# Attention inside a gate projection: transposes of p three steps behind their scores, pv products four, with a fifth buffer for p

## The chip, the cores and the metric

The kernel runs on one core of one Trainium2 chip. The metric is the device time of one execution in microseconds (us). The times shown are the median, lowest and highest of three executions; a profile was taken of one execution.

## The reference, cut to what matters

One layer of an encoder, for a prompt of 1024 rows and a sample of 64 rows (1088 rows in all, model width 1024, 8 heads of width 64). Only the attention matters here:

```python
def mixer(xn, conv_prefix, attn_fn, w_in, w_conv, w_conv_out, w_attn_out, w_out):
    proj = xn @ w_in
    cb, cc, ch, q, k, v, ga, gb = jnp.split(proj, ...)
    ya = (cb * causal_conv(cc * ch)) @ w_conv_out
    o = attn_fn(heads(q), heads(k), heads(v))
    yb = o.reshape(B, L, ATT_DIM) @ w_attn_out
    merged = jax.nn.sigmoid(ga) * ya + jax.nn.sigmoid(gb) * yb
    return merged @ w_out, ...

def band_attend(q, k, v, q_pos, k_pos, rel_bias):
    s = jnp.einsum('bqhd,bkhd->bhqk', q, k) * (HEAD_DIM ** -0.5)
    allowed = ...          # own chunk of 64 rows and the 8 chunks before it
    s = jnp.where(allowed, s + bias, NEG_INF)
    p = jax.nn.softmax(s, axis=-1)
    return jnp.einsum('bhqk,bkhd->bqhd', p, v)
```

A SwiGLU feed-forward part follows; the change does not touch it.

## The kernel before, in words

Every product is made from two halves of each operand (a high part and a low part in a reduced 32-bit format), so that a product of 128 contraction rows costs three matmuls (L333, L334, L335). The part of the program that the change touches has two streams of work, which share TensorE (PE).

The first stream is the gate projections `g`: ten blocks of 128 columns, each in four pieces of 272 rows, 24 matmuls of 128x272 a piece. Their sums are copied out by ScalarE (ACT, L815) and stored.

The second is the attention, a Python generator of steps. A step is one tile of one head: 8 heads with 9 tiles each (t = 0 to 7 are 128 rows of the prompt, t = 8 is the 64 rows of the sample), so 72 steps in the order (0,0), (0,1) ... (7,8). In this text `s5_6` is the scores of head 5, tile 6, `t5_6` the transposes of the same tile, and s_0 or t_7 means that tile in any head. A step's work:

- `scores` (L892 on): the matmuls L907 and L908 into the PSUM tile `s`; VectorE (DVE, L865) adds the bias, writes the sum to the SBUF tile p and finds its extreme in one pass; ScalarE (L875) makes the exponential in place in p and adds up its rows. A tile has 128 (t = 0), 256, 384, 512 or 640 columns (t = 4 to 7), and 576 for the sample.
- `transposed` (L920 on): TensorE transposes p, 128 columns at a time, into a PSUM tile `t` (L954; L926 and L929 for the sample). ScalarE copies it out as the high part of `pt` (L128), VectorE subtracts to get the low part (L129), and with that the PSUM buffer is free. For t = 8 the reciprocal of the head's row sums follows (L935) and a transpose of it, `rt` (L937).
- `values` (L958 on): for each pair of tiles the products with v, `pv` (L979, and L966 for the sample), copied and added up (L881 to L883) and stored in `o_d` by a DMA (L886).

The scores, the transposes and `rt` take their PSUM tiles from one pool, `patt`, with two buffers in all (the tag "att"). The gates have three PSUM banks of their own, pv one. The SBUF tile p rotates through four buffers.

How far the three parts of a step lie apart is set in `attention` (L1007 on): turn i of its loop issues the scores of step i, the transposes of step i-2 and the pv products of step i-3. `between()` runs after each gate piece and takes 3.15 turns on average (PER). Before the last two gates, `for _ in steps: pass` (L1061) takes all turns that are left; then the attention's pools are closed and the loads of `u` and the output of the attention (`ob`, L1072 to L1088) are issued, whose products `ya` and `yb` come behind the last gate. A scheduler then orders the instructions of each engine by its own estimate of times; that is why the orders below are not simply those of the code. Once ordered, each engine takes its instructions strictly in that order.

Of the kernel before, what the change touches and what calls it, by code (L numbers as in the profile page):

```python
# [8 lines left out]
F32 = mybir.dt.float32  # L9
# [6 lines left out]
P = 128  # L16
# [50 lines left out]
def encoder_kernel(ctx: ExitStack, tc: tile.TileContext, ins, outs):  # L67
# [58 lines left out]
    def split(hi, lo, src):  # L126

        a = act.copy(hi, src)  # L128
        b = vec.tensor_tensor(lo, src, hi.bitcast(F32), op=ALU.subtract)  # L129
        return a.ins, b.ins  # L130
# [626 lines left out]
    for n in range(len(units)):  # L757
# [21 lines left out]
        for _ in r:  # L779
            if n < 2 and si in (2 + n, 5 + n):  # L780
                i = 2 * n + si // 5
# [23 lines left out]
    at_pool = att_stack.enter_context(tc.tile_pool(name="at_pool", bufs=2, reuse_waits="tile"))  # L805
# [24 lines left out]
    def head_load(h):  # L830
        q = []
        for l in range(2):
            qq = qp.tile([P, T], F32R, tag=f"q{l}", name=f"qd{h}_{l}", bufs=2 + l)
            for j in range(2):
                nc.sync.dma_start(qq[j * HD : (j + 1) * HD].bitcast(F32), q_d[h, :, l])
            q.append(qq)
        k = hd_pool.tile([P, TP], F32R, tag="k", name=f"kd{h}")
        ks = hd_pool.tile([P, CACHE + TS], F32R, tag="ks", name=f"ksd{h}", bufs=1)

        for l in range(2):  # L840
            ls = slice(l * HD, (l + 1) * HD)
            src = k_d[h, :, l]
            for e in range(2):
                nc.sync.dma_start(k[ls, 512 * e : 512 * e + 512].bitcast(F32), src[:, 576 * e : 576 * e + 512])
            nc.sync.dma_start(ks[ls, :CACHE].bitcast(F32), src[:, T:])
            nc.sync.dma_start(ks[ls, CACHE:].bitcast(F32), src[:, 512:576])
        v = hd_pool.tile([P, 8, P], F32R, tag="v", name=f"vd{h}")
        nc.sync.dma_start(v.bitcast(F32), v_d[h, :TP].rearrange("(b p) e -> p b e", p=P))
        vs = hd_pool.tile([P, 5, P], F32R, tag="vs", name=f"vsd{h}", bufs=1)
        nc.sync.dma_start(vs[:, :4].bitcast(F32), v_d[h, TP : TP + CACHE].rearrange("(b p) e -> p b e", p=P))  # L850
        nc.sync.dma_start(vs[:TS, 4].bitcast(F32), v_d[h, TP + CACHE :])
        b = bb[:, h % 2]
        near = bias_d[h, 127 : 127 + P * 383].rearrange("(p n) -> p n", n=383)
        far = bias_rows(h, 0, 384)
        nc.sync.dma_start(b[:HD, :384], far[:HD])
        nc.sync.dma_start(b[HD:, HD:384], far[HD:, HD:])
        nc.sync.dma_start(b[:HD, 384:576], near[:HD, :192])
        nc.sync.dma_start(b[HD:, 384:], near[HD:, :256])
        heads[h] = (q, k, ks, v, vs, b)

    def softmax(s, ps, bias, sm, nm):

        rows = s.shape[0]
        mx = at_pool.tile([P, 1], F32, tag="mx", name=f"mx{nm}", bufs=3)[:rows]
        vec.tensor_tensor_reduce(  # L865
            out=s if len(ps.shape) == 2 else s.rearrange("p (a b) -> p a b", a=2),
            in0=ps,
            in1=bias if len(ps.shape) == 2 else bias.rearrange("p (a b) -> p a b", a=2),
            scale=-1.0,
            scalar=3e38,  # L870
            op0=ALU.add,
            op1=ALU.min,
            accum_out=mx,
        )
        act.activation(s, s, AF.Exp, bias=mx, scale=-1.0, accum_out=sm)  # L875
# [16 lines left out]
    def scores(h, t):  # L892
        q, k, ks, v, vs, bias = heads[h]
        ps = patt.tile([P, 2, 512], F32, tag="att", name=f"s{h}_{t}")
        s = at_pool.tile([P, 640], F32, tag="s", name=f"p{h}_{t}", bufs=4)
        if t < 8:
            nb = min(t + 1, 5)
            k0, n, r = (t - nb + 1) * P, nb * P, P
            q0 = t * P if t < 4 else t * P + TS
        else:  # L900
            k, k0, n, r = ks, 0, CACHE + TS, TS
            q0 = 512
        parts = 2 if n > 512 else 1
        w = n // parts
        for i in range(parts):
            ksl = slice(k0 + i * w, k0 + (i + 1) * w)
            mm(ps[:r, i, :w], q[0][:, q0 : q0 + r], k[:, ksl], start=True, stop=False)  # L907
            mm(ps[:r, i, :w], q[1][:, q0 : q0 + r], k[:, ksl], start=False, stop=True)  # L908
        b0 = 640 - n if t < 8 else 0
        if t == 0:  # L910
            sums[h] = sm2[:, h % 2]
        sm = sums[h]
        softmax(
            s[:r, :n], ps[:r, :, :w] if parts == 2 else ps[:r, 0, :w], bias[:r, b0 : b0 + n], sm[:r, t : t + 1],
            f"{h}_{t}",
        )
        return s
# [3 lines left out]
    def transposed(h, t, s):  # L921
        tp = patt.tile([P, 2, 512], F32, tag="att", name=f"t{h}_{t}").rearrange("p a b -> p (a b)")
        if t == 8:
            pt = at_pool.tile([P, 2, 5, TS], F32R, tag="pts", name=f"pts{h}", bufs=1)
            for i in range(4):
                nc.tensor.transpose(  # L926
                    tp[:, i * TS : (i + 1) * TS], s[:TS, i * P : (i + 1) * P], ident[:TS, :TS]
                )
            nc.tensor.transpose(tp[:TS, 512 : 512 + TS], s[:TS, 512:576], ident[:TS, :TS])  # L929
            split(pt[:, 0, :4, :], pt[:, 1, :4, :], tp[:, : 4 * TS].rearrange("p (b t) -> p b t", t=TS))  # L930
            split(pt[:TS, 0, 4, :], pt[:TS, 1, 4, :], tp[:TS, 512 : 512 + TS])
            pts[h, 4] = pt

            sm = sums.pop(h)
            vec.reciprocal(sm, sm)  # L935
            tr = patt.tile([P, 2, 512], F32, tag="att", name=f"rt{h}")[:9, 0, :P]
            nc.tensor.transpose(tr, sm, ident)  # L937
            rows = at_pool.tile([P, P], F32, tag="rows", name=f"rows{h}", bufs=1)[:9]
            act.copy(rows, tr)
            for e in range(2):  # L940
                nc.gpsimd.dma_start(
                    rc_d[h, e * HT : e * HT + 512].rearrange("(t p) -> t p", p=P), rows[4 * e : 4 * e + 4]
                )
                c = e * HT + 512
                nc.gpsimd.dma_start(rc_d[h : h + 1, c : c + 32], rows[8:9, 32 * e : 32 * e + 32])
            return
        g, j = divmod(t, 2)
        if j == 0:
            pts[h, g] = at_pool.tile([P, 2, 6, 256], F32R, tag="pt", name=f"pt{h}_{g}")
        pt = pts[h, g]  # L950
        nb = min(t + 1, 5)
        b0 = t - nb + 1 - max(0, 2 * g - 4)
        for i in range(nb):
            nc.tensor.transpose(tp[:, i * P : (i + 1) * P], s[:, i * P : (i + 1) * P], ident)  # L954
        src = tp[:, : nb * P].rearrange("p (b t) -> p b t", t=P)
        js = slice(j * P, (j + 1) * P)
        split(pt[:, 0, b0 : b0 + nb, js], pt[:, 1, b0 : b0 + nb, js], src)
# [49 lines left out]
    def attention():  # L1007
        order = [(h, t) for h in range(NH) for t in range(9)]
        done = []
        for i in range(len(order) + 3):  # L1010
            if i < len(order):
                h, t = order[i]
                if t == 3 and h + 1 < NH:
                    head_load(h + 1)
                if h + 1 == NH and t in (3, 5):
                    o_early(t // 4)
                done.append(scores(h, t))
            if 0 <= i - 2 < len(order):
                transposed(*order[i - 2], done[i - 2])
            if i >= 3:  # L1020
                h, t = order[i - 3]
                if t % 2 or t == 8:
                    values(h, t)
            yield
# [34 lines left out]
    for i in range(4, len(GATES)):  # L1059
        gate_w[i] = next_w()  # L1060
        if i == len(GATES) - LAST:  # L1061
# [5 lines left out]
            for nm, pad in (("u", 56), ("ob", 48)):  # L1067
                uo.tile([P, pad], F32, name=f"pad_{nm}")
                t = uo.tile([P, 2, 4 * T + 8], F32R, name=nm)[:, :, : 4 * T]
# [27 lines left out]
    for m0 in range(0, 8, 2):  # L1097
        for m in (m0, m0 + 1):
# [3 lines left out]
            for o, n in PIECES:  # L1102
                t = sg["ga", m, o]
# [5 lines left out]
        for m in (m0, m0 + 1):  # L1109
# [3 lines left out]
            for o, n in PIECES:  # L1113
                t, z = sg.pop(("ga", m, o)), sg.pop(("gb", m, o))
# [7 lines left out]
                h, a = o // HT, 512 - o % HT  # L1122
# [468 lines left out]
    order = [(i + 4 * h, d) for g in range(2) for h, d in ((0, 0), (1, 0), (1, 1), (0, 1)) for i in (2 * g, 2 * g + 1)]  # L1591
    homes = [(hp, "snap")] * 3 + [(hp0, "snap"), (hp0, "sa")] + [(hp, "sa")] * 4 + [(hp, "hs")]
    bufs = {(hp, "hs"): 1, (hp, "snap"): 3, (hp, "sa"): 4, (hp0, "snap"): 1, (hp0, "sa"): 1}
    for n, (i, d) in enumerate(order):
        if n < len(homes):
            pool, tag = homes[n]
# [28 lines left out]
    for b, ks in enumerate(blocks):  # L1625
        first, final = b == 0, b == len(blocks) - 1
        nk = blocks[b + 1] if not final else []
        for g in range(2):
# [28 lines left out]
            for si, js in turns:  # L1657
                p, ht = STEPS[si], hts[base + si]
                key = {1: "A", 6: "A", 5: "A", 3: "A", 2: "B", 7: "D", 4: "D"}[p]
                for j in js:  # L1660
                    i = 2 * g + j
                    if (key, j) not in ps:
                        ps[key, j] = psD.tile(
                            [P, 512], F32, tag="A" if key == "A" else "BD", name=f"{key}{b}_{i}",
                            bufs=2 if key == "A" else 4,
                        )
                    t = ps[key, j]
                    for k, kp in enumerate(ks):
# [7 lines left out]
                    h, d, fresh = {  # L1676
                        1: (0, 0, 1), 2: (0, 0, 0), 6: (1, 0, 1), 7: (1, 1, 1), 5: (1, 1, 0), 4: (1, 0, 0), 3: (0, 1, 1),
                    }[p]
# [79 lines left out]
```

## Time and profile before

| | |
|---|---|
| time, median of 3 (lowest to highest) | 1472.06 us (1471.79 to 1472.19) |
| the profiled execution: own time, span | 1471.79 us, 1469.7 us |
| mean granted TensorE clock of that execution | 0.998 |
| busy in the span: PE, DVE, ACT, POOL | 1455.4, 984.1, 679.9, 136.5 us |
| first scores, first gate matmul behind the last pv | 370.20 us, 551.00 us |
| first `ya` matmul, first `yb` matmul | 571.82 us, 583.84 us |

The page gives, for one execution, the busy time of each engine and its share of the span, the span in 40 slices, the chain of work that ended last, and the costliest groups of instructions. The trace behind it gives each instruction with its start, its duration and what ended the idle time ahead of it. Matmuls are pipelined, so their durations overlap; what a matmul costs is read from the distance of two starts.

### The profile page before, as it was taken

The page shows a single profiled execution, that of the slowest core. Times are in us where ns is not written, and L with a number is a line of the kernel's source. Part 1 is how long each engine was busy: PE and PEld are TensorE (multiplying, and loading weights), DVE is VectorE, ACT ScalarE, POOL GpSimd, SP SyncE. Part 2 cuts the span into 40 slices and gives each one's busy share as a digit, 9 for nine tenths or more (in the row PEclk, how much of TensorE's full clock was granted, in tenths as well). Part 3 has the DMA queues.
Part 4 walks back from the last instruction along what each step waited for, and adds up shares of the span by engine and source line. Part 5 has one row for each costly group of instructions (what it writes and reads, how often), then busy time and mean ns, then how long its engine had stood idle before and what let it go on. Part 6 is the DMA issues. An engine that isn't in the chain of part 4 may idle for free.

```text
span 1469.7 us, 26408 instructions
## 1 busy us (share of the span) xinstructions
PE 1455.4 (99%) x10176; PEld 1366.7 (93%) x10176; DVE 984.1 (67%) x1856; ACT 679.9 (46%) x1391; POOL 136.5 (9%) x249
## 2 busy tenths in 40 slices
PE   9999999999999999999999999999999999999997
PEld 6899999999989899998889999999999999888886
DVE  7975465641677775763588767766666768957676
ACT  7654433422777776531355444444444445512223
POOL 1400010001111111000100111110011111000000
PEclk9999999999999999999999999999999999999999
DMA  8686522237776757534432443443344449877675
GB/s 285 181 277 225 178 88 88 66 115 228 209 193 179 182 168 244 164 119 136 154 108 80 153 168 139 168 151 123 122 152 168 147 166 303 287 233 239 223 268 205
DMA packets 163134, 260.26 MB, mean 177 GB/s; under 512 B 18785, under 2 KB 98849, under 8 KB 163009
## 3 DMA queue, kind: packets, MB, share of 16 engines
q1 hardware_dynamic: 142080, 192.79, 42.1%
q0 software_dynamic: 19776, 63.70, 12.1%
q10 hardware_dynamic: 1152, 2.10, 0.4%
q8 instruction: 80, 1.31, 0.4%
q14 instruction: 46, 0.37, 0.1%
HBM read 170.67 MB, written 89.70 MB: 177 GB/s over the span
## 4 chain that ended last, share of the span: by engine, by line
PE 94%; DVE 3%; ACT 1%; DMA 1%; issue 1%; SPq 0%; ACTq 0%; DVEq 0%
PE Ab L269 9%; PE Aa L269 8%; PE A L1671 8%; PE Db L269 4%; PE Da L269 4%; PE D L1671 4%; PE g L335 3%; PE g L334 3%; PE g L333 3%; PE Agb L269 2%; PE B L1671 2%; PE wo L1163 2%; PE Bb L269 2%; PE Ba L269 2%; PE wo L1165 2%; PE wo L1164 2%
## 5 line engine op out<-in xcount | busy, mean ns | idle before, releaser
L333 PE MATMUL g<-xn,wp 128*128 128x272 f32 x320 | 93.7, 293 | 0.0
L335 PE MATMUL g<-xn,low 128*128 128x272 f32 x320 | 93.4, 292 | 0.0
L334 PE MATMUL g<-xn,wp 128*128 128x272 f32 x320 | 92.7, 290 | 0.0
L128 ACT CAST ring<-w2r 128x512 fp32r<-128x512 f32 (+1 forms) x78 | 43.2, 588 | 97.9 <-PE A L1671 49.9
L865 DVE CUSTOM_DVE_ANT_0 p<-s,bb 128x640 f32<-128x640 f32 (+5 forms) x72 | 47.4, 660 | 38.5 <-PE s L908 37.2
L1671 PE MATMUL A<-ring,low 128*128 128x512 f32 x264 | 72.4, 389 | 0.0
L1671 PE MATMUL A<-ring,ht 128*128 128x512 f32 x264 | 72.4, 390 | 0.0
L129 DVE TENSOR_TENSOR low<-rawa,wa 128x512 fp32r<-128x512 f32 x55 | 37.7, 687 | 41.4 <-ACT wa L128 41.4
L335 PEld LDWEIGHTS g<-xn,low 128*128 128x128 f32 x320 | 60.3, 189 | 0.5
L333 PEld LDWEIGHTS g<-xn,wp 128*128 128x128 f32 x320 | 60.3, 189 | 0.5
L334 PEld LDWEIGHTS g<-xn,wp 128*128 128x128 f32 x320 | 60.2, 188 | 0.5
L1671 PEld LDWEIGHTS A<-ring,low 128*128 128x128 f32 x264 | 49.6, 188 | 10.4
L1671 PEld LDWEIGHTS A<-ring,ht 128*128 128x128 f32 x264 | 49.3, 188 | 10.6 <-ACT acc L1681 0.6
L269 PE MATMUL Aa<-tt,wa 128*128 128x272 f32 x352 | 57.8, 285 | 0.9 <-ACT sa_Q L257 0.9
L269 PE MATMUL Aa<-mg,wa 128*128 128x272 f32 x352 | 57.8, 286 | 0.5 <-DVE sa L1324 0.5
L269 PE MATMUL Ab<-mg,wb 128*128 128x272 f32 x352 | 57.9, 285 | 0.0
L129 DVE TENSOR_TENSOR ring<-w2r,ring 128x512 fp32r<-128x512 f32 (+1 forms) x78 | 48.9, 645 | 13.4 <-ACT ring L128 13.4
L269 PE MATMUL Ab<-tt,wb 128*128 128x272 f32 x352 | 57.8, 286 | 0.0
L875 ACT ACTIVATE p<-p,mx 128x640 f32<-128x640 f32 (+5 forms) x72 | 50.8, 706 | 11.5 <-DVE mx L865 10.2
L128 ACT CAST wa<-rawa 128x512 fp32r<-128x512 f32 x55 | 34.0, 621 | 47.4 <-PE Ab L269 33.3
L128 ACT CAST wb<-rawb 128x512 fp32r<-128x512 f32 x55 | 33.9, 621 | 38.8 <-PE Aa L269 24.5
L1163 PE MATMUL wo<-low,mg 128*128 128x512 f32 x128 | 50.9, 397 | 0.0
(551 smaller groups left out, 4547.8 us busy)
## 6 DMA issues: line engine op xcount, KB each, us to landing
h_d<-hq POOLq DMA_DIRECT2D x44, 512.0 KB, 4.7
ht<-h_d SPq DMA_DIRECT2D x77, 256.0 KB, 3.6
low<-h_d SPq DMA_DIRECT2D x77, 256.0 KB, 3.9
h_d<-hq_early POOLq DMA_DIRECT2D x29, 512.0 KB, 5.0
rawa<-in_w_ff SPq DMA_DIRECT2D x11, 1024.0 KB, 6.4
rawb<-in_w_ff SPq DMA_DIRECT2D x11, 1024.0 KB, 5.4
w2r<-in_w_ff SPq DMA_DIRECT2D x11, 1024.0 KB, 7.9
qd<-q_d SPq DMA_DIRECT2D x32, 272.0 KB, 4.3
```

The lines of the kernel that those rows point to most:

```text
L128: a = act.copy(hi, src)
L129: b = vec.tensor_tensor(lo, src, hi.bitcast(F32), op=ALU.subtract)
L269: newest[0] = mm(t[:, j, :HN], w[:, k, :], x[p][:, k, l, j * HN : (j + 1) * HN], start=p in (1, 2, 7) and k == 0 and n == 0, stop=k == 3 a ...
L333: mm(out, a, first, start=k == 0, stop=False)
L334: mm(out, a, then, start=False, stop=False)
L335: mm(out, b, p, start=False, stop=k == kt - 1)
L865: vec.tensor_tensor_reduce(out=s if len(ps.shape) == 2 else s.rearrange("p (a b) -> p a b", a=2), in0=ps, in1=bias if len(ps.shape) == 2 e ...
L875: act.activation(s, s, AF.Exp, bias=mx, scale=-1.0, accum_out=sm)
L1163: mm(ps, x(k, 0), wh, start=f, stop=False)
L1164: mm(ps, x(k, 1), wh, start=False, stop=False)
L1165: mm(ps, x(k, 0), wl, start=False, stop=e)
L1671: mm(t, ht[k][:, j, x], w[:, l], start=p in (1, 2, 7) and k == 0 and n == 0, stop=k == len(ks) - 1 and n == 2, skip_group_check=p in (6, 5 ...
```

## The change

The transposes of p move from two turns behind their scores to three, and the pv products from three to four. The loop has one turn more, so the generator has one more to give before it is empty. The pool of p has five buffers in place of four.

```diff
     def scores(h, t):
         q, k, ks, v, vs, bias = heads[h]
         ps = patt.tile([P, 2, 512], F32, tag="att", name=f"s{h}_{t}")
-        s = at_pool.tile([P, 640], F32, tag="s", name=f"p{h}_{t}", bufs=4)
+        s = at_pool.tile([P, 640], F32, tag="s", name=f"p{h}_{t}", bufs=5)
...
     def attention():
         order = [(h, t) for h in range(NH) for t in range(9)]
         done = []
-        for i in range(len(order) + 3):
+        for i in range(len(order) + 4):
             if i < len(order):
...
                 done.append(scores(h, t))
-            if 0 <= i - 2 < len(order):
-                transposed(*order[i - 2], done[i - 2])
-            if i >= 3:
-                h, t = order[i - 3]
+            if 0 <= i - 3 < len(order):
+                transposed(*order[i - 3], done[i - 3])
+            if i >= 4:
+                h, t = order[i - 4]
                 if t % 2 or t == 8:
                     values(h, t)
             yield
```

Each engine has the same instructions in both programs. TensorE's order differs from the first turns of the attention to the last gates. The place that the prediction speaks of most is the end of head 5, where head 6 begins. In the rows, the name left of the arrow is the tile that is written and those right of it the tiles that are read; the number behind the last underscore only tells tiles apart, and x5 means five such instructions in a row. On TensorE before, from the transposes of t5_5 to the scores s6_1 (left out are ten g matmuls and three of the four of s5_8):

```order
L954 MATMUL t5_5_5774<-ident_75,p5_5_5721 128x128 x5
...
L908 MATMUL s5_8_5810<-ksd5_5312,qd5_1_5308 64x288
L333 MATMUL g6_2_5896<-xn01_99,wp6_0_5206 128x272
L334 MATMUL g6_2_5896<-xn01_99,wp6_0_5206 128x272
L954 MATMUL t5_6_5819<-ident_75,p5_6_5737 128x128 x5
L979 MATMUL pv5_5_5828<-pt5_2_5746,vd5_5321 128x512 x4
L979 MATMUL pv5_5_5828<-pt5_2_5746,vd5_5321 128x2x128 x2
L907 MATMUL s6_0_5841<-kd6_5630,qd6_0_5624 128x128
L908 MATMUL s6_0_5841<-kd6_5630,qd6_1_5627 128x128
L335 MATMUL g6_2_5896<-xn01_99,low_95 128x272
L954 MATMUL t5_7_5848<-ident_75,p5_7_5766 128x128 x5
L907 MATMUL s6_1_5856<-kd6_5630,qd6_0_5624 128x256
```

The same place of TensorE in the changed program (left out are four g matmuls ahead of s6_0 and six behind it):

```order
L954 MATMUL t5_5_5811<-ident_75,p5_5_5705 128x128 x5
...
L907 MATMUL s6_0_5819<-kd6_5612,qd6_0_5606 128x128
L908 MATMUL s6_0_5819<-kd6_5612,qd6_1_5609 128x128
...
L954 MATMUL t5_6_5826<-ident_75,p5_6_5730 128x128 x5
L979 MATMUL pv5_5_5835<-pt5_2_5755,vd5_5303 128x512 x4
L979 MATMUL pv5_5_5835<-pt5_2_5755,vd5_5303 128x2x128 x2
L907 MATMUL s6_1_5848<-kd6_5612,qd6_0_5606 128x256
L908 MATMUL s6_1_5848<-kd6_5612,qd6_1_5609 128x256
L334 MATMUL g6_2_5863<-xn01_99,wp6_0_5198 128x272
L335 MATMUL g6_2_5863<-xn01_99,low_95 128x272
L333 MATMUL g6_2_5863<-xn11_100,wp6_4_5201 128x272
L954 MATMUL t5_7_5855<-ident_75,p5_7_5746 128x128 x5
```

The scores of head 6 have moved one place ahead against the transposes of head 5: s6_0 stands before t5_6, and between t5_6 and t5_7 there are now s6_1 and three g matmuls in place of s6_0 and one. Between t5_5 and t5_6, where sixteen matmuls of s5_8 and g stood, there are ten of g and two of s6_0.

On VectorE the same place before, where L865 is the pass over scores, L129 the subtraction that frees a buffer of `t`, L935 the reciprocal of the sums of head 5 and L882 part of pv's sum:

```order
L129 TENSOR_TENSOR pt5_2_5746<-t5_5_5774,pt5_2_5746 128x5x128
L865 ISA p5_8_5811,mx5_8_5816<-s5_8_5810,bb_3689 64x576
L865 ISA mx5_8_5816 64x1
L129 TENSOR_TENSOR pt5_3_5820<-t5_6_5819,pt5_3_5820 128x5x128
L935 RECIPROCAL sm2_3694<-sm2_3694 128x9
L865 ISA p6_0_5842,mx6_0_5845<-s6_0_5841,bb_3689 128x128
L865 ISA mx6_0_5845 128x1
L882 TENSOR_TENSOR ca5_2_5835<-pv5_5_5828,ca5_2_5835 64x512
```

and in the changed program:

```order
L865 ISA p5_8_5803,mx5_8_5808<-s5_8_5802,bb_3689 64x576
L865 ISA mx5_8_5808 64x1
L883 TENSOR_TENSOR co5_1_5769<-ca5_1_5768 64x256
L129 TENSOR_TENSOR pt5_2_5755<-t5_5_5811,pt5_2_5755 128x5x128
L865 ISA p6_0_5820,mx6_0_5823<-s6_0_5819,bb_3689 128x128
L865 ISA mx6_0_5823 128x1
L935 RECIPROCAL sm2_3694<-sm2_3694 128x9
L129 TENSOR_TENSOR pt5_3_5827<-t5_6_5826,pt5_3_5827 128x5x128
```

The subtraction for t5_6 has moved behind the scores of s6_0 and behind the reciprocal, which it stood ahead of.

## The prediction

> **What bounds the kernel now.** I read the page first, then what the transposes and the scores wait for (the view of one source line and of one tile), then TensorE's timeline around the head boundaries, and last the stretch behind the attention. The page says that TensorE sets the time:
>
> ```profile
> span 1469.7 us, 26408 instructions
> PE 1455.4 (99%) x10176; PEld 1366.7 (93%) x10176; DVE 984.1 (67%) x1856; ACT 679.9 (46%) x1391; POOL 136.5 (9%) x249
> PEclk9999999999999999999999999999999999999999
> ```
>
> TensorE is busy for 99% of the span, with the granted clock at 90% of full speed or more in every slice, and the change takes no matmul away and adds none. So it can only change what TensorE waits, and only where its order changes: in the attention and the gates that run with it. How much waiting there is, is told by two views. The first is of the transposes, source line L954, the second of the tiles `s` between 370 and 552 us; "us, times" follows each releaser:
>
> ```profile
> its engine sat idle before it (us, times) until:
>   DVE pt L129: 3.3, 12
> ```
>
> ```profile
>   DVE mx L865: 2.4, 10
> ```
>
> Transposes wait 3.3 us for the subtraction that frees a PSUM buffer of `t`, scores 2.4 us for the VectorE pass that frees a buffer of `s`: 5.7 us in all, in 22 places. The views put these under VectorE and its queue, and no wait of a transpose on the exponential appears. The end of head 5 shows how such a wait comes about; these rows are TensorE's:
>
> ```profile
> 497.64 0.71 PE L954 MATMUL t<-ident,p 128*128 128x128 f32 x5
> 498.10 1.42 PE L979 MATMUL pv<-pt,vd 128*128 128x512 f32 x6
> 499.36 0.22 PE L907 MATMUL s<-kd,qd 128*128 128x128 f32 x1
> 499.53 0.34 PE L335 MATMUL g<-xn,low 128*128 128x272 f32 x1
> 500.04 0.76 PE L954 MATMUL t<-ident,p 128*128 128x128 f32 x5 [0.17 <-DVE pt L129]
> 500.56 0.36 PE L907 MATMUL s<-kd,qd 128*128 128x256 f32 x1
> 500.88 0.28 PE L333 MATMUL g<-xn,wp 128*128 128x272 f32 x1
> ```
>
> and these are ScalarE's and VectorE's:
>
> ```profile
> 497.12 0.19 ACT L875 ACTIVATION_READ_ACCUMULATOR p<-p,mx 128x1 f32 x1
> 498.44 0.69 ACT L128 CAST pt<-t 128x640 fp32r<-128x640 f32 x1 [0.84 <-PE t L954]
> 499.16 0.82 DVE L129 TENSOR_TENSOR pt<-t,pt 128x640 fp32r<-128x640 f32 x1 [0.82 <-ACT pt L128]
> 499.93 0.21 DVE L935 RECIPROCAL sm<-sm 128x9 f32<-128x9 f32 x1
> ```
>
> The second row of transposes is t5_7. Its data were ready early: the last part of its exponential, the accumulator's read, ended at 497.12 + 0.19 = 497.31, 2.7 us before 500.04. It stood until t5_6 left its PSUM buffer: transposed from 497.64, copied by 499.13, subtracted by 499.98. From the first instruction behind t5_6 (498.10) to t5_7 that is 1.94 us; I call this the release. Behind t5_6 TensorE had six pv products and s6_0 (to 499.53) and one gate matmul. A gate matmul costs 0.125 us (166 of them fill the 20.82 us from 551.00 to 571.82, quoted below). So work was there for 1.43 + 0.125 = 1.555 us and the wait was 0.385.
>
> **The change part by part.**
>
> *The distance from scores to transposes.* One turn more gives the exponential about 2.5 us more (a turn is 180.8 us / 72, from the first scores at 370.20 to 551.00). The row of t5_7 shows that it did not need them. Worth nothing. The fifth buffer keeps the slack that p's buffers had: four buffers with transposes two turns behind, five with three. Nothing either way.
>
> *t_7 behind t_6.* The same short stretch, with one gate matmul or few behind t_6, recurs:
>
> ```profile
> 433.09 0.34 PE L334 MATMUL g<-xn,wp 128*128 128x272 f32 x1
> 433.61 0.55 PE L954 MATMUL t<-ident,p 128*128 128x128 f32 x3 [0.18 <-DVE pt L129]
> 478.41 0.29 PE L335 MATMUL g<-xn,low 128*128 128x272 f32 x1
> 478.80 0.44 PE L954 MATMUL t<-ident,p 128*128 128x128 f32 x2
> 522.14 0.34 PE L333 MATMUL g<-xn,wp 128*128 128x272 f32 x1
> 522.66 0.44 PE L954 MATMUL t<-ident,p 128*128 128x128 f32 x2 [0.18 <-DVE pt L129]
> ```
>
> Start to start less 0.125, heads 2, 4 and 6 wait 0.395, 0.265 and 0.395 us; with head 5, 1.44 us. In the changed order six pv products (498.10 to 499.36, 1.26 us), s_1 (0.24 to 0.32: twice 0.12, or 500.56 to 500.88) and three gate matmuls (0.375) stand there in heads 0, 1, 4, 5 and 6, more in the others: 1.88 to 1.96 us against a release of 1.94, a wait of 0 to 0.07 in five heads. I take 0.2 in all. **Gain 1.2 us.**
>
> *t_6 behind t_5.* Here the work shrinks: before, sixteen matmuls of s_8 and gates in head 5. Now heads 1, 4, 5 and 6 have 13, 11, 10 and 12 gate matmuls (1.625, 1.375, 1.25, 1.5 us) and s_0 (0.17: 499.36 to 499.53). Against 1.94 that leaves waits of 0.15, 0.40, 0.52 and 0.27, 1.34 us in all. The release of 1.94 was counted from a slow first pv product, whose wait for its weights the gate matmuls would meet too, so perhaps 0.1 less each, 0.9. **Cost 1.2 us** (0.9 to 1.4).
>
> *s_1 behind s_0.* Before, they stand close in heads 1 and 2:
>
> ```profile
> 389.77 0.37 PE L333 MATMUL g<-xn,wp 128*128 128x272 f32 x1
> 390.31 0.38 PE L907 MATMUL s<-kd,qd 128*128 128x256 f32 x1 [0.17 <-DVE mx L865]
> 411.92 0.73 PE L954 MATMUL t<-ident,p 128*128 128x128 f32 x5
> 412.52 0.39 PE L907 MATMUL s<-kd,qd 128*128 128x256 f32 x1
> ```
>
> Less the work (one gate matmul, 0.125; five transposes, 0.46 from 497.64 to 498.10) s_1 waits 0.415 and 0.14. In the changed order all of t_6 and more stands between. **Gain 0.55 us.**
>
> *s_2 behind s_1.* The new close pair: in heads 3 and 4 only five transposes (t_7) stand between. The reduce is longer,
>
> ```profile
> L865 DVE CUSTOM_DVE_ANT_0 p<-s,bb 128x128 f32<-128x128 f32 x8 | 2.3, 283 | 26.2 <-PE s L908 26.2
> L865 DVE CUSTOM_DVE_ANT_0 p<-s,bb 128x256 f32<-128x256 f32 x8 | 3.3, 414 | 0.3 <-PE s L908 0.3
> ```
>
> by 0.13 us, so that the 0.60 us of head 2 become 0.73 and the wait 0.27, twice. **Cost 0.55 us** (0 if s_2 takes the other buffer in time; 1.0 if the other heads' pairs, some gate matmuls apart, wait as well).
>
> *s_3 behind s_2.* In heads 2 and 6, s_3 waits for the reduce of s_2; head 6's:
>
> ```profile
> 506.19 0.54 DVE L865 CUSTOM_DVE_ANT_0 p<-s,bb 128x384 f32<-128x384 f32 x1
> 506.79 0.50 PE L907 MATMUL s<-kd,qd 128*128 128x512 f32 x1
> ```
>
> s6_3 starts 0.06 us behind the reduce's end. In the changed order it takes the buffer that t_8 and `rt` left earlier. At the mean of the recorded waits of scores (2.4 / 10) twice: **gain 0.5 us** (0 to 0.5).
>
> *Everything else.* The remaining places of the 22 are shuffled in the same way (t_1, t_2, t_8, s_4); I count them at nothing, with an error of about 1 us to both sides. The head loads are queued on SP in the same turns, h+1 at t = 3, and that stays so.
>
> *The tail.* The last pv products stand later: behind them are 153 gate matmuls ahead of `ya`, 166 before.
>
> ```profile
> 551.00 0.39 PE L335 MATMUL g<-xn,low 128*128 128x272 f32 x1
> 571.82 0.29 PE L333 MATMUL ya<-u,wp 128*128 128x272 f32 x1
> 564.48 1.29 DVE L129 TENSOR_TENSOR u<-u 128x1088 fp32r<-128x1088 f32 x1 [0.31 <-ACT u L128]
> 583.84 0.29 PE L333 MATMUL yb<-ob,wp 128*128 128x272 f32 x1
> 575.41 1.28 DVE L129 TENSOR_TENSOR ob<-rc,ob 128x1088 fp32r<-128x1088 f32 x1
> ```
>
> The attention's end and all that hangs on it (the stores of `o_d` by SP, the loads of `u`, its split and that of `ob`) come 13 x 0.125 = 1.6 us nearer to their readers. The last split of `u` ends at 565.77, 6.0 us ahead of `ya`; that of `ob` at 576.69, 7.1 us ahead of `yb`. Cover of 4.4 and 5.5 us is left. Cost nothing; with the cover gone each us of delay would be a us of the end.
>
> *The sum:* -1.2 + 1.2 - 0.55 + 0.55 - 0.5 = -0.5 us. The profiled execution took 1471.79 us, 2.1 more than its span and 0.3 less than the median of the runs; the same sum at the median gives 1472.06 - 0.5 = **1471.6 us**.
>
> **The rivals.**
>
> *The waits only move (no change, 1472.1).* The same wait, t_7's, returns in most heads at the engine that is otherwise full, and what ends it is the release of a PSUM buffer; there are two, and the change adds none. Then what goes at one boundary returns at the next. For it: the terms above nearly cancel as they stand. The Trainium skill, page "Perfetto Trace Analysis", section "Optimization Strategy", says of consistent bubbles on the engine that should be saturated that they can mean that SBUF or PSUM has no room for the next tile; here the trace agrees with its 12 waits on L129, and by that rule a buffer more of p, which nothing waits for, brings nothing.
>
> *Faster (1468).* About half of the waiting goes: the 5.7 us recorded and 22 restarts of 0.1 us (a matmul behind a wait starts late; my estimate from 500.04 to 500.56, where five transposes take 0.52 in place of 0.46, as a lower end) make 8 us; half is 4. It decides where the release is shorter than 1.94: at 1.4 no t_6 waits, and t_7 doesn't either. For it: a turn more of distance loosens what the scheduler may set between two uses of a buffer. Against it: the release is 0.8 us from the transposes' start to the copy, 0.69 of copy and 0.82 of subtraction without a queue between them.
>
> *Slower (1476).* VectorE becomes late. In the changed order the reciprocal of the sums stands ahead of the subtraction for t_6 and no longer behind it; it waits for the exponential of s_8, and all of VectorE behind it waits too. Before, it did so in three heads, by the view of its line L935:
>
> ```profile
>   ACT p L875: 2.7, 3
> ```
>
> 0.9 us each. If that falls into the release of t_6, t_7 waits 0.07 + 0.9 in five heads, 4.8 us, in place of 1.4; the other terms add 0.7 (1.2 - 0.55 + 0.55 - 0.5): 4.1 us, 1476.2. It decides from a stall of about 0.7 us. Against it: s_8 itself stands a place earlier against t_6 than before, so its exponential should be done; and in head 5 the row of the reciprocal shows no idle time ahead of it even now.
>
> **How the numbers follow.** 0.2% is 2.9 us, about what a measurement of this kernel can tell from no change: faster means below 1469.1, slower above 1475.0. The forecast with its re-sorted waits gets 0.28, the case that they only move 0.20, faster 0.33, slower 0.19. The first two lie within 0.2%, with their error of 1 us and the bounds of the terms (1470 to 1473.5). So faster 0.33, the same 0.48, slower 0.19. The range reaches down to 1467.0, where five of the eight us are gone, and up to 1476.0, just short of the slower case: outside is about a third of each side's case, 0.1 below and 0.1 above.
>
> **What would show it.** In the changed kernel's trace: transposes still idle for L129, but ahead of t_6 in heads 1, 4, 5 and 6 (0.1 to 0.5 us each) and hardly ahead of t_7; no wait of s_1 in heads 1 and 2, one of s_2 in heads 3 and 4; `ya` still without a wait, about 19 us behind the last pv; the release of t_6 at 1.9 to 2.0 us. The forecast is wrong if the idle time before L954 and `s` sums to under 2 us or over 8, if the reciprocal's wait stands ahead of a late subtraction, or if TensorE's time changes outside 370 to 572 us.

## The result, and the profile after

| | before | changed |
|---|---|---|
| median of 10 runs each (lowest to highest) | 1471.91 us (1471.41 to 1473.26) | 1474.35 us (1473.47 to 1477.11) |
| ratio, 95% interval | | 1.0021 (1.0013 to 1.0029) |
| profiled execution: own time, span | 1471.79, 1469.7 us | 1474.19, 1472.2 us |

The changed kernel is 2.4 us slower, and its runs spread over 3.6 us. In a second set of runs on another chip (e5 below) it was 1.0015 (1.0006 to 1.0024); one run of that set, of 3715.44 us, is marked slow and left out of the ratio.

The page of the changed kernel has the same picture as before, TensorE busy to 99% and at full clock, and a span longer by 2.5 us:

```profile
span 1472.2 us, 26378 instructions
PE 1456.8 (99%) x10176; PEld 1367.2 (93%) x10176; DVE 983.0 (67%) x1856; ACT 678.5 (46%) x1391; POOL 136.0 (9%) x249
```

Where it lies is told by three points of TensorE's timeline: the first scores, the first `ya` matmul (start, duration) and, by subtraction, what is outside.

```profile
370.15 0.22 PE L907 MATMUL s<-kd,qd 128*128 128x128 f32 x1
574.49 0.29 PE L333 MATMUL ya<-u,wp 128*128 128x272 f32 x1
```

From the first scores to `ya` it is 204.34 us, against 571.82 - 370.20 = 201.62 before: 2.7 us, all of the difference. Within that stretch, the views of source line L954 and of the tiles `s`, read as those of before:

```profile
its engine sat idle before it (us, times) until:
  DVE pt L129: 5.7, 8
```

```profile
  DVE mx L865: 2.1, 9
```

These views, here and in the prediction, add up two kinds of rows of TensorE: matmuls, and the loads of their weights, which the profile lists apart (PEld). One wait can stand in both, as that of t5_7 before does:

```profile
500.04 0.53 PEld L954 LDWEIGHTS t<-ident,p 128*128 128x128 f32 x5 [0.38 <-DVE pt L129]
500.04 0.76 PE L954 MATMUL t<-ident,p 128*128 128x128 f32 x5 [0.17 <-DVE pt L129]
```

So their sums, the prediction's 5.7 us in 22 places among them, count some waits twice and are no lengths of time. By the matmul rows alone transposes waited for L129 as follows, before and in the changed kernel (us, times, longest):

```profile
PE t L954 <- DVE pt L129: 0.7, 4, 0.2
PE t L954 <- DVE pt L129: 2.3, 2, 2.0
```

That is fewer places, as was expected, but more time. One wait makes it. TensorE, in head 6: t6_4, the last gate matmul behind it, and t6_5.

```profile
516.76 0.71 PE L954 MATMUL t<-ident,p 128*128 128x128 f32 x5
520.15 0.29 PE L335 MATMUL g<-xn,low 128*128 128x272 f32 x1
522.48 0.77 PE L954 MATMUL t<-ident,p 128*128 128x128 f32 x5 [2.04 <-DVE pt L129]
```

From the start of t6_4 to that of t6_5 it is 5.7 us, where the same two lay 2.4 us apart before (514.96 to 517.37). With 0.125 us for the gate matmul at 520.15, work was there until 520.28, so that the wait is 2.2 us. The reason stands on ScalarE, whose copy of t6_4 (520.90) is the first step of the release, and VectorE's subtraction only follows it:

```profile
516.29 0.19 ACT L875 ACTIVATION_READ_ACCUMULATOR p<-p,mx 128x1 f32 x1
519.55 0.62 ACT L128 CAST wp<-rawp 128x512 fp32r<-128x512 f32 x1 [3.08 <-DMA rawp<-in_w_conv_out]
520.08 0.82 ACT L875 ACTIVATE p<-p,mx 128x640 f32<-128x640 f32 x1
520.90 0.67 ACT L128 CAST pt<-t 128x640 fp32r<-128x640 f32 x1
...
521.60 0.82 DVE L129 TENSOR_TENSOR pt<-t,pt 128x640 fp32r<-128x640 f32 x1 [0.70 <-ACT pt L128]
```

ScalarE stood for 3.08 us ahead of a conversion that has nothing to do with attention: the weights `wp10`, for the first `ya` products some 55 us later, whose load (`rawp`, 512 KB of w_conv_out) had not landed. The copy of t6_4 was queued behind it. SyncE's rows say why it hadn't: in the changed kernel the load is issued at 512.89, directly behind the early read of `o_d` (L1003),

```profile
512.21 0.58 SPq L1003 DMA_DIRECT2D o<-o_d  x1
512.89 0.38 SPq L301 DMA_DIRECT2D rawp<-in_w_conv_out  x1
```

while before it was issued 19.5 us earlier, among the stores of head 5, and ScalarE came to the conversion 18.5 us later without a wait:

```profile
493.39 0.53 SPq L301 DMA_DIRECT2D rawp<-in_w_conv_out  x1
...
511.89 1.13 ACT L128 CAST wp<-rawp 128x512 fp32r<-128x512 f32 x2
```

In SyncE's order the load went from place 271 of the queue to 294; ScalarE's conversion went from ahead of the copy of t6_3 to ahead of that of t6_4. The diff touches neither.

Of the re-sorted waits, that of t_7 in head 5 went as expected, and that of t_6 is smaller than expected. Head 5 in the changed kernel, from the last gate matmul ahead of t5_6 to t5_7:

```profile
499.49 0.29 PE L333 MATMUL g<-xn,wp 128*128 128x272 f32 x1
499.68 0.77 PE L954 MATMUL t<-ident,p 128*128 128x128 f32 x5
500.20 1.42 PE L979 MATMUL pv<-pt,vd 128*128 128x512 f32 x6
501.94 0.29 PE L333 MATMUL g<-xn,wp 128*128 128x272 f32 x1
502.14 0.55 PE L954 MATMUL t<-ident,p 128*128 128x128 f32 x3
```

t5_7 starts 0.20 us behind the start of the last gate matmul, a wait of 0.075 in place of 0.385; the release, 500.20 to 502.14, is again 1.94. t5_6 starts 0.19 us behind the gate matmul ahead of it, a wait of 0.065 where 0.52 was expected.

### The profile page after: what moved, and what is told of

Same layout as the page of the kernel before. It is cut to its first block, busy times and chain, and to the rows that moved or that the text cites. A ratio compares the mean times of both kernels' runs of the same rounds, so it can differ in the third digit from the quotient of the medians.

```text
span 1472.2 us, 26378 instructions
## 1 busy us (share of the span) xinstructions
PE 1456.8 (99%) x10176; PEld 1367.2 (93%) x10176; DVE 983.0 (67%) x1856; ACT 678.5 (46%) x1391; POOL 136.0 (9%) x249
## 4 chain that ended last, share of the span: by engine, by line
PE 93%; DVE 2%; DMA 2%; ACT 1%; SPq 1%; issue 0%; ACTq 0%; DVEq 0%
PE Ab L269 9%; PE Aa L269 8%; PE A L1671 8%; PE Db L269 4%; PE Da L269 4%; PE D L1671 4%; PE Agb L269 2%; PE Bb L269 2%; PE Ba L269 2%; PE wo L1163 2%; PE B L1671 2%; PE wo L1165 2%; PE wo L1164 2%; PE g L334 2%; PE g L333 2%; PE g L335 2%
## 5 line engine op out<-in xcount | busy, mean ns | idle before, releaser
L865 DVE CUSTOM_DVE_ANT_0 p<-s,bb 128x640 f32<-128x640 f32 (+5 forms) x72 | 47.5, 661 | 39.2 <-DMA qd<-q_d 26.2
L129 DVE TENSOR_TENSOR low<-rawa,wa 128x512 fp32r<-128x512 f32 x55 | 37.7, 686 | 41.0 <-ACT wa L128 41.0
L129 DVE TENSOR_TENSOR ring<-w2r,ring 128x512 fp32r<-128x512 f32 (+1 forms) x78 | 48.8, 646 | 12.6 <-ACT ring L128 12.6
L129 DVE TENSOR_TENSOR pt<-t,pt 128x640 fp32r<-128x640 f32 (+2 forms) x64 | 41.6, 651 | 16.0 <-ACT pt L128 15.7
```

Source lines behind the costliest of these rows:

```text
L865: vec.tensor_tensor_reduce(out=s if len(ps.shape) == 2 else s.rearrange("p (a b) -> p a b", a=2), in0=ps, in1=bias if len(ps.shape) == 2 e ...
```

## The experiments

Theory A: the late weight load makes ScalarE stand, and the release of a PSUM buffer stands behind it. Theory B: the re-sorted waits on PSUM buffers at the head boundaries are what costs. All runs of the first four were made on one chip beside 33 runs of the kernel before (median 1471.82 us), those of the last four on another beside 33 (1471.67 us); 11 runs of each kernel.

**e1, the load early again.** Nothing of the change is undone; the two weight loads are only requested earlier in the program.

```diff
+                if (h, t) == (6, 0):
+                    plain_load(8)
+                    plain_load(10)
                 if t == 3 and h + 1 < NH:
                     head_load(h + 1)
```

> The changed kernel, with the loads of the two weight blocks that follow (among them the 512 KB of w_conv_out for the first ya products) requested in the program at the turn of step (6,0), so that SyncE issues the second of them in head 5, as in the kernel before, and not behind the early read of o_d. Theory A (the late load makes ScalarE stand at the conversion of these weights, and the copy of t6_4 with its PSUM buffer stands behind it): the 2.2 us wait ahead of t6_5 goes, 1474.35 - 2.2 = 1472.2 us (1471.6 to 1472.7), and the runs lie within 1 us of each other in place of 3.6. Theory B (the waits on PSUM buffers at the head boundaries, re-sorted by the change, cost the 2.4 us): nothing of this changes, 1474.3 us.

Measured: 1472.10 us, ratio to before 1.0005 (0.9996 to 1.0014). In its profile the load is issued at 492.07, ScalarE doesn't wait for it, and t6_5 starts as soon as the work ahead is done. The view of L954, and the wait by its matmul rows alone:

```profile
  DVE pt L129: 1.4, 6
PE t L954 <- DVE pt L129: 0.3, 1, 0.3
```

and the timeline's rows of SyncE, ScalarE and TensorE:

```profile
492.07 0.53 SPq L301 DMA_DIRECT2D rawp<-in_w_conv_out  x1
...
511.73 1.28 ACT L128 CAST wp<-rawp 128x512 fp32r<-128x512 f32 x2
...
520.29 0.29 PE L908 MATMUL s<-ksd,qd 128*64 128x288 f32 x1
520.43 0.39 PE L954 MATMUL t<-ident,p 128*128 128x128 f32 x2
```

The 2.2 us are gone with the transposes where the change puts them: A holds, B falls as the main cause. TensorE's order is that of the changed kernel for the first 1051 of the 1440 matmuls from the first scores to `ya`, up to 519.9 us; behind that some stand elsewhere, such as three gate matmuls that were ahead of t6_5. The mean granted clock of this profile is 0.948, where the others have 0.998 or 0.999, but from `ya` to the end it takes 897.9 us as the kernel before does, so that the clock does not bear on the times. The spread was not as narrow as expected: 9 of 11 runs lie within 1.2 us, two at 1474.15 and 1476.11, and the kernel before had such runs beside it too (up to 1474.84).

**e2, the load late, but the conversion behind the copy of t6_7.**

```diff
+        if i == 9:
+            plain_load(10)
+            with tc.issue_after(cast_of[6, 7]):
+                gate_w[i] = next_w()
```

> The changed kernel with the load left late, but ScalarE's conversion of these weights held back until behind its copy of t6_7. Theory A in its narrow form (only what is queued behind the conversion on ScalarE is hurt): 1472.2 us (1471.6 to 1472.8), no wait over 0.5 us ahead of t6_5. If instead the late load hurts by its own traffic or by making the ya products late: 1474 us or more, with a wait at ya or at the transfers. Theory B: 1474.3 us.

Measured: 1473.24 us, 1.0010 (1.0001 to 1.0018), outside the expected range. The wait ahead of t6_5 went, as the narrow form says, but half of the gain came back as another wait of the same kind. On VectorE, the multiplication of the early `o` rows waits for its DMA, the pass over scores behind it is late, and with it the buffer for the scores that follow:

```profile
536.51 1.29 DVE L1006 TENSOR_TENSOR o<-o,rc 128x1088 f32<-128x1088 f32 x1 [0.93 <-DMA rc<-rc_d]
...
539.19 0.42 PE L907 MATMUL s<-kd,qd 128*128 128x320 f32 x1 [0.91 <-DVE mx L865]
```

**e3, the kernel before, with that load made late.**

```diff
+        if i == 9:
+            with tc.issue_after(o_ld[0]):
+                plain_load(10)
         gate_w[i] = next_w()
```

> The kernel before, distances two and three, with that one load issued behind the early read of o_d, as the changed kernel has it. Theory A: the conversion stands on ScalarE behind the exponential of (6,6) and ahead of the copy of t6_5; issued near 514.0 us and landing 6 to 7 us later it holds ScalarE for 2 to 4 us, and TensorE waits 1 to 2.5 us ahead of t6_6: 1473 to 1474.5 us, with runs spread over more than 1.5 us. Theory B: 1471.9 us, no change.

Measured: 1473.43 us, 1.0010 (1.0002 to 1.0019), 1.6 us above the kernel before by the medians. ScalarE waits for the load, and TensorE ahead of t6_6; the rows of SyncE, ScalarE and TensorE, and the first `ya`:

```profile
514.17 0.54 SPq L301 DMA_DIRECT2D rawp<-in_w_conv_out  x1
...
518.84 0.62 ACT L128 CAST wp<-rawp 128x512 fp32r<-128x512 f32 x1 [0.71 <-DMA rawp<-in_w_conv_out]
...
521.91 0.77 PE L954 MATMUL t<-ident,p 128*128 128x128 f32 x5 [0.75 <-DVE pt L129]
...
370.17 0.22 PE L907 MATMUL s<-kd,qd 128*128 128x128 f32 x1
572.95 0.29 PE L333 MATMUL ya<-u,wp 128*128 128x272 f32 x1
```

So the late load slows the kernel without any of the change's distances (behind 520.3 us TensorE's order differs a little here too). In the profiled run ScalarE stood for less than expected (0.71 us for 2 to 4), as the load was there 4.7 us after its issue and not after 6 to 7. The stretch to `ya` is 202.78 us, 1.2 more than before; the rest of this run's 2.0 us of span (1471.7 for 1469.7) lies behind `ya`, 0.7 of it near 1250 us in the feed-forward part, which nothing ties to this load.

**e4, transposes three turns behind, pv products three.**

```diff
-        for i in range(len(order) + 4):
+        for i in range(len(order) + 3):
...
-            if i >= 4:
-                h, t = order[i - 4]
+            if i >= 3:
+                h, t = order[i - 3]
```

> Half of the change: transposes three turns behind their scores, pv products three as before, five buffers for p. In this program the weight load stands far ahead on SyncE, in head 3. Theory A: no wait of ScalarE for that load; re-sorted waits only, 1471.5 to 1472.8 us. Theory B (the transposes' new place is what costs): 1474 us.

Measured: 1474.98 us, 1.0018 (1.0009 to 1.0027): the time that B gives, but not for its reason. TensorE's matmul rows show a single wait of 0.2 us in the attention, and the long one at its end: only 56 gate matmuls are left behind the last pv, and `u`, whose load and split come when the attention's pools are closed, is late.

```profile
571.32 0.29 PE L335 MATMUL g<-xn,low 128*128 128x272 f32 x1
573.19 0.39 PE L333 MATMUL ya<-u,wp 128*128 128x272 f32 x1 [1.59 <-ACT u L128]
```

1.87 us between the two starts, and 0.9 more in the `ya` products behind it. This is the cover of the tail that the prediction put at 153 gate matmuls for the change; here it is gone. The profiled execution (1473.71 us) lies 1.3 us below the median of these runs, so what the slower ones add is not shown.

**e5, the changed kernel again, and e8, the same with four buffers for p.**

```diff
-        s = at_pool.tile([P, 640], F32, tag="s", name=f"p{h}_{t}", bufs=5)
+        s = at_pool.tile([P, 640], F32, tag="s", name=f"p{h}_{t}", bufs=4)
```

> The changed kernel once more, on the chip and beside the runs of the kernels of this row, so that they can be compared with it directly. All theories: 2.0 to 2.8 us above the kernel before.

> The changed kernel with four buffers for p in place of five; TensorE's order is the same. If the fifth buffer does nothing (the prediction): the same as the changed kernel within 0.7 us, and no wait of VectorE on a transpose. If it carries the change: scores wait for the transposes that free p, 1 us or more slower.

Measured: 1473.84 us for e5, 1.0015 (1.0006 to 1.0024), and 1473.86 us for e8, 1.0018 (1.0009 to 1.0027). The fifth buffer does nothing, as predicted. TensorE's order in the stretch to `ya` is the same in both as in the profile above. Their profiles give the same stall in two more sizes; ScalarE's wait and TensorE's, of e5

```profile
518.59 0.62 ACT L128 CAST wp<-rawp 128x512 fp32r<-128x512 f32 x1 [2.22 <-DMA rawp<-in_w_conv_out]
521.52 0.77 PE L954 MATMUL t<-ident,p 128*128 128x128 f32 x5 [1.20 <-DVE pt L129]
```

and of e8:

```profile
519.27 0.62 ACT L128 CAST wp<-rawp 128x512 fp32r<-128x512 f32 x1 [2.50 <-DMA rawp<-in_w_conv_out]
522.20 0.77 PE L954 MATMUL t<-ident,p 128*128 128x128 f32 x5 [1.52 <-DVE pt L129]
```

With the profile above, ScalarE waits 2.22, 2.50 and 3.08 us for the same load, and TensorE 1.20, 1.52 and 2.04: 1.0 us less each time. That 1.0 us is the slack that the release had: work behind t6_4 lasted from 517.23 to 520.28 in the profile above, 3.05 us, and a release takes 1.94, which leaves 1.1. Past it, each us of ScalarE's wait is about one of the stretch to `ya` (203.47, 203.94 and 204.34 us). The slack belongs to this order: in e3 0.71 us of ScalarE's wait went with 0.75 of TensorE's. That the spread of the runs comes from the same load is likely but not shown, as only the profiled executions have a trace; e1, without the stall, spread no less.

**e6 and e7, transposes two turns behind, pv products four; e7 with the load early as in e1.**

```diff
-            if 0 <= i - 3 < len(order):
-                transposed(*order[i - 3], done[i - 3])
+            if 0 <= i - 2 < len(order):
+                transposed(*order[i - 2], done[i - 2])
```

> The other half of the change: transposes two turns behind their scores as before, pv products four, four buffers for p. In this program the weight load stands on SyncE behind the early read of o_d, and ScalarE's conversion of it ahead of its copy of t6_5, as in the kernel before with the load made late. Theory A: a wait of 1 to 2.5 us ahead of t6_5 or t6_6, 1.0 to 2.5 us slower than the kernel before. Theory B (what costs is the transposes' distance of three): within 0.7 us of the kernel before.

> The same with the weight loads requested at the turn of step (6,0): SyncE issues the load of w_conv_out some 20 places ahead of the early read of o_d. Theory A: the wait goes, 0.8 to 2 us less than with the load late, within 0.7 us of the kernel before. If the pv products' distance costs by itself: no difference between the two.

Measured: e6 1472.72 us, 1.0005 (0.9996 to 1.0013); e7 1472.25 us, 1.0006 (0.9997 to 1.0014). The expected loss of e6 did not come clearly. The load is late there too, but in the profiled run it landed almost in time; SyncE and ScalarE:

```profile
511.75 0.38 SPq L301 DMA_DIRECT2D rawp<-in_w_conv_out  x1
...
516.53 0.62 ACT L128 CAST wp<-rawp 128x512 fp32r<-128x512 f32 x1 [0.34 <-DMA rawp<-in_w_conv_out]
```

ScalarE waits 0.34 us, and in this profile no transpose's matmul waits more than 0.2 us for L129. But the profiled execution (1471.39 us) is one of the fastest of its eleven, 1.3 us below their median, so the slower ones may have had the stall. The pair is inconclusive on A; it shows that pv four turns behind costs by itself no more than 0.14%, the upper end of e7's interval.

## Why the prediction was wrong, point by point

It forecast 1471.6 us, 0.5 us less than before, and the kernel is slower by 0.21% in the first set of runs and 0.15% in the second, both intervals clear of zero. The step that failed is "Everything else": there it says that the head loads are queued on SP in the same turns "and that stays so", and counts nothing for the rest. That looks at SyncE's queue for one kind of load and leaves out the others. The weight load for `ya` was moved 23 places back in that queue, past stores to `o_d`, head loads (most of them head 7's) and the early read of `o_d`, and ScalarE's order was not looked at for what stands between two copies of transposes. The missing term is 2.2 us (e1: 1472.1 with it taken away, against 1474.35), more than the error of 1 us that was allowed for, and e3 makes 1.6 us of it in the kernel before by the medians, 1.2 of them in the stretch to `ya`. The prediction's own signs of being wrong did not show: the two views sum to 7.8 us, short of its 8, the reciprocal is not late, and the loss lies inside 370 to 575 us.

The terms that were worked out, each by the distance of two starts in both profiles. A figure for all heads is the sum of such waits: the distance less the usual one of the same two kinds of matmul, for which the lower quartile in the ten profiles is taken.

- *Distance from scores to transposes, fifth buffer:* nothing, right (e8).
- *t_7 behind t_6:* gain 1.2 expected; in head 5 the wait goes from 0.385 to 0.075, in all heads from 1.56 to 0.38. Right.
- *t_6 behind t_5:* cost 1.2 expected, 0.52 of it in head 5. There the release is 1.89 us (497.79 to 499.68), as expected, but the wait came in two pieces: 0.165 already at s6_0, whose buffer the pass over s_8 had not left, and 0.065 at t5_6. Heads 1, 4, 5 and 6 wait 0.06, 0.20, 0.06 and 0.07 us where 0.15, 0.40, 0.52 and 0.27 were expected: right in kind, and much too high. Head 0, where no wait was expected, has the largest, 0.435 us (388.26 to 388.82 less 0.125): on ScalarE a conversion of gate weights and an exponential stand ahead of the copy of t0_5, as it looks a small case of the same stall, without a load to wait for. With it all heads come to 1.1 us, for 0.1 before; that the sum is near 1.2 is luck.

```profile
497.79 0.37 PE L333 MATMUL g<-xn,wp 128*128 128x272 f32 x1
498.25 0.29 PE L333 MATMUL g<-xn,wp 128*128 128x272 f32 x1
498.54 0.33 PE L907 MATMUL s<-kd,qd 128*128 128x128 f32 x1
...
388.26 0.28 PE L334 MATMUL g<-xn,wp 128*128 128x272 f32 x1
388.82 0.30 PE L954 MATMUL t<-ident,p 128*128 128x128 f32 x1 [0.28 <-DVE pt L129]
...
385.71 0.62 ACT L128 CAST wp<-rawp 128x512 fp32r<-128x512 f32 x1
387.12 0.69 ACT L128 CAST pt<-t 128x640 fp32r<-128x640 f32 x1
```

- *s_2 behind s_1:* 0.27 expected in heads 3 and 4; both wait 0.22. In head 3, s_2 starts 0.69 us behind the transposes; less 0.46 that is 0.23. Right:

```profile
435.57 0.71 PE L954 MATMUL t<-ident,p 128*128 128x128 f32 x5
436.26 0.44 PE L907 MATMUL s<-kd,qd 128*128 128x384 f32 x1
```

- *s_1 and s_3:* gains of 0.55 and 0.5 expected. The waits ahead of s_1 went from 0.55 us to nothing, those of s_3 from 0.57 to nothing. Right, but for s_3 partly by luck: heads 2 and 6 had 0.08 and 0.14 in place of 0.24 each, and four other heads the rest.
- *The tail:* 153 gate matmuls behind the last pv, `ya` without a wait. Right; e4 shows what it costs where the cover is gone.
- *The faster rival:* its 8 us were the views' 5.7, which count waits twice, and 22 restarts of 0.1 us. By the starts all waits ahead of scores and transposes come to 6.2 us before.
- *The reciprocal (the slower rival):* it didn't become late (its idle time for the exponential, 2.7 us in 3 places before, is 0.3 in one); what made ScalarE and with it VectorE late was the weight conversion. The rival had the right shape, a stall ahead of a release, and the wrong instruction: it searched for it on VectorE alone and among the attention's own steps.
- *The rule of the Trainium skill* (page "Perfetto Trace Analysis", section "Optimization Strategy": repeated bubbles on the engine that should be full can mean that SBUF or PSUM has no room for the next tile): the small waits that end with a release in PSUM, before and after, are of the kind that it names, and the fifth buffer of p brought nothing; no run adds a PSUM buffer, so the rule itself is not tested. The wait that decided ended with the same PSUM release, but a buffer was not what it lacked: with the load early it was gone with two buffers.

Taken alone, the new order with the load early (e1) costs between -0.6 and +2.1 us by the interval; -0.5 was forecast. In e1's profile the stretch from the first scores (370.46) to `ya` (572.90) is 202.44 us, 0.8 more than before; that execution lies 0.7 us above e1's median and the one before 0.1 below its own, so this is no more than runs differ. The starts of its matmuls say where it lies. Ahead of all scores and transposes TensorE waits 4.8 us by the count above, for 6.2 before: 1.4 us less, more than the forecast's 0.5. But the other matmuls of the stretch (pv products, the second halves of scores, gates) start later by 2.2 us in all, mostly in pieces of under 0.15 us, and that side of a new order was not priced. Why they start later stays open. So does the reason why the scheduler set the load back: it moved with the pv products' distance in e6 as well, but with three and three (e4) it went forward to head 3.

No version here beats the kernel before by more than its runs differ.

## What to carry to other kernels

A change to the turns of one stream moves every instruction that the scheduler places around it, also those of the next stage. Before such a change is costed, go through the orders of all queues for the loads that moved back, and for each its first reader: what is queued behind that reader on its engine, and whose buffer waits for that. Here ScalarE, busy to 46%, was the place where a late load stopped TensorE, busy to 99%; in e2 it was VectorE, busy to 67%.

## What the runs showed of the hardware

The 512 KB load took from 4.7 us (e3, issued 514.17, read at 518.84) to 6.7 us (the changed kernel, issued 512.89, read at 519.55) from its issue to the conversion that waits for it. Three executions of the changed order, with TensorE's instructions in the same sequence, had 5.8 (e5, issued 512.79, read at 518.59), 6.2 (e8, issued 513.10, read at 519.27) and 6.7 us; where the load is what ScalarE waits for, the stretches of the three to `ya` differ by as much, 0.9 us.
